# A PEER decoder block: the second product's sums added two PSUM banks at a time, the gate matrix in 8 KB rows and ended earlier, expert numbers and residual moved, 28 lead tiles

## The chip, the cores and the metric

The kernel runs on one core of a Trainium2 chip. The metric is the device time of one execution in microseconds (us); three executions of the kernel before took 3583.12, 3585.42 and 3587.71 us, a median of 3585.42.

## What is computed

One decoder block on 512 tokens of width 2048: two gated token mixers, then a layer of 16384 experts of one neuron each, of which every token takes 8 x 16. The change touches the expert layer, so that part of the reference is shown.

```
def block(xb):                                   # tokens in blocks of 128
    q = (xb @ w_q).reshape(PEER_TOKEN_BLOCK, PEER_HEADS, 2, PEER_HALF)
    s = jnp.einsum('thcd,hcnd->thcn', q, sub_keys).astype(jnp.float32)
    s_top, i_top = lax.top_k(s, PEER_TOPK)
    cand = s_top[:, :, 0, :, None] + s_top[:, :, 1, None, :]
    cand_idx = i_top[:, :, 0, :, None] * PEER_KEYS + i_top[:, :, 1, None, :]
    ...
    best, pos = lax.top_k(cand, PEER_TOPK)
    expert = jnp.take_along_axis(cand_idx, pos, axis=-1)
    gates = jax.nn.softmax(best, axis=-1).astype(xb.dtype)
    u_sel = u_tab[expert]
    v_sel = v_tab[expert]
    act = jax.nn.gelu(jnp.einsum('td,thkd->thk', xb, u_sel))
    return jnp.einsum('thk,thkd->td', gates * act, v_sel)
...
h = rmsnorm(x, norm_ffn[l])
x = x + peer(h, ...)
return rmsnorm(x, norm_final)
```

## The kernel before

**Two ways through the experts.** Of the 512 tokens 160 (GA = 128 and GB = 32) get their experts by row gathers: POOL issues an indirect transfer of one expert row for each of 128 tokens (L963, 1 MB), DVE multiplies and sums it (L1011 for u, L1022 for v, "row" below). The other ND = 352 tokens are computed densely against all 16384 experts, in 128 tiles of 128 experts. Products in float32 are made of three: each weight piece is split by `split` (L204, L205) into a high part, copied by ACT, and a low part, subtracted on DVE or on POOL ("a split" below), and PE adds high x low, high x high and low x high.

**First product.** `dense_u(j)` computes u of tile j: 16 slices x 3 = 48 matmuls of 352 columns into a PSUM bank (L235 to L237), then ACT's gelu (L862) gives ga. The weights of a tile come in two pieces, and so in two splits. For tiles under UPOOL = 10 both are on POOL, later ones on DVE.

**Lead tiles and gate steps.** The first LEAD = 24 tiles are computed ahead; their ga goes to DRAM (d_ga) and comes back later as gar. Meanwhile the gates become a dense matrix. After tile LAG - 1 = 5, `transp_routes` runs the softmax over the scores and turns the chosen expert numbers and gates; from tile LAG on, `gate_steps` issues 88 steps of four tokens. A step is oi and oj on DVE (comparisons of 128 x 512, L892, L898), the multiplication of oi by the gate (every third step on POOL, L894, else on ACT, L897), four token matmuls on PE (L907), and two copies by ACT into a staging tile (L910). After 32 tokens two transfers of 1 MB write the staging tiles to d_g (SP's queue, L913). The steps are spaced so that they end TAIL tiles before the lead does. `pump_rows` issues steps of the row gathers between tiles: RLEAD for each lead tile from LAG + 4 on, RV for each block without a first product.

**Expert numbers.** `expert_ids` makes the numbers (eid) on DVE, after the last top-16. `spread` carries those of the 32 tokens over to 128 partitions: a transfer to d_eb and four back, all on POOL's queue (L823, L825), and likewise the gates through d_gb.

**Second product.** 32 groups of four tiles. `weigh` multiplies ga by the gate: gq is loaded by POOL's queue (L1073), POOL multiplies (L1081), and the result is split into wh (ACT) and wl (DVE). `dense_v(g, dc, ws)` computes one of four blocks dc of the group: 48 matmuls (L1130 to L1132) into four PSUM banks pv, which DVE adds to acc in SBUF one by one (L59, 128 x 352). The pool of pv has six banks. acc begins as the residual, loaded from d_x2 by SP in group 0 (L1120). As long as the tiles of the next group are lead tiles, a group consists of second products only: 20 blocks, of groups 0 to 4. From then on one first product and one block take turns. In the last group `turn_out` turns acc back by transposes into pv banks, ACT squares, DVE multiplies, and `finish` normalises.

**What sets the order.** The program is written engine by engine by a scheduler of the language, which takes instructions by its own estimates of when they can run; `issue_after` ties some to an earlier instruction. Each engine then runs its instructions in the built order, and one that waits holds all that stand behind it. Matmuls, splits and DMA issues stand in such queues, POOL's included.

## Time and profile before

| | |
|---|---|
| median of three executions | 3585.42 us (3583.12 to 3587.71) |
| the profiled execution | 3586.99 us, its span 3584.8 us, mean granted clock 0.98 |
| PE busy | 3416.8 us, 95% |
| DVE busy | 2856.6 us, 80% |
| ACT busy | 1281.7 us, 36% |
| POOL busy | 1452.8 us, 41% |

The times of the stages are counted from the start of the span. PE, DVE, ACT and POOL are the engines for matmuls, vectors, activations and GpSimd; SP only issues transfers. The mixers end about 1330 us; the first product starts before the routing on DVE ends. The gate steps lie between 1434 and 1650 us, the second product starts at 1686 us, and the groups with second products only last until 1897 us. PE records overlap, since matmuls are pipelined: the distance of their starts is what one costs.

### The profile page before, as it was taken

What the parts mean: (1) busy time and instruction counts of PE and PEld (TensorE: products, weight loads), DVE (VectorE), ACT (ScalarE), POOL (GpSimd) and SP (SyncE); (2) the same over time, 40 slices, a digit from 0 to 9 for tenths busy, and PEclk for the clock granted to TensorE, in tenths of its full rate; (3) what the DMA queues carried; (4) which work ended last, traced back from release to release, by engine and by line L of the source; (5) the groups of instructions that cost most, each with busy time, mean ns of one, the idle gap of its engine ahead of it and who ended that gap; (6) DMA issues with size and microseconds to landing.
All of it is one profiled execution on the core that took longest, in us unless ns stands there. A gap on an engine that the chain in (4) does not pass through costs nothing. (4 is left out here: it accounts for less than half of the span.)

```text
span 3584.8 us, 50132 instructions
## 1 busy us (share of the span) xinstructions
PE 3416.8 (95%) x19091; PEld 3169.5 (88%) x19091; DVE 2856.6 (80%) x4147; ACT 1281.7 (36%) x2025; POOL 1452.8 (41%) x924
## 2 busy tenths in 40 slices
PE   8999999999999994997889999999999999999998
PEld 6888888888888884986789999999999999999998
DVE  7685848996535997796866999978999898797984
ACT  4234344325223331873223333333333333433333
POOL 1200000110003543343654666656666666465642
PEclk9999999999999997998899999999999999999999
DMA  5533444434444332699877989898989889897882
GB/s 176 154 108 114 129 123 123 140 125 129 135 147 132 113 111 69 188 302 320 273 252 264 357 333 355 340 337 317 356 347 343 335 342 358 285 361 295 344 303 95
DMA packets 261905, 845.30 MB, mean 236 GB/s; under 512 B 42640, under 2 KB 105184, under 8 KB 219904
## 3 DMA queue, kind: packets, MB, share of 16 engines
q1 hardware_dynamic: 189248, 433.25, 35.9%
q0 software_dynamic: 64352, 396.12, 29.4%
q10 hardware_dynamic: 8064, 12.72, 1.0%
q8 instruction: 150, 2.46, 0.3%
q14 instruction: 91, 0.75, 0.1%
HBM read 790.91 MB, written 51.09 MB: 235 GB/s over the span
## 5 line engine op out<-in xcount | busy, mean ns | idle before, releaser
L204 ACT CAST whi<-wraw 128x1024 fp32r<-128x1024 f32 x736 | 771.9, 1051 | 1792.1 <-PE pu L236 610.5
L205 DVE TENSOR_TENSOR wlo<-wraw,whi 128x1024 fp32r<-128x1024 f32 x556 | 743.1, 1351 | 207.6 <-ACT whi L204 206.5
L237 PE MATMUL pu<-h2h,wlo 128*128 128x352 f32 x2048 | 664.9, 325 | 67.7 <-POOL wlo L205 50.6
L1130 PE MATMUL pv<-wh,whi 128*128 128x352 f32 x2048 | 671.1, 328 | 47.8 <-DVE acc L59 29.9
L1132 PE MATMUL pv<-wh,wlo 128*128 128x352 f32 x2048 | 667.5, 326 | 4.7 <-DVE wlo L205 4.7
L235 PE MATMUL pu<-h2l,whi 128*128 128x352 f32 x2048 | 670.1, 327 | 1.1 <-ACT whi L204 1.1
L1131 PE MATMUL pv<-wl,whi 128*128 128x352 f32 x2048 | 667.5, 326 | 0.0
L236 PE MATMUL pu<-h2h,whi 128*128 128x352 f32 x2048 | 660.2, 322 | 0.0
L205 POOL TENSOR_TENSOR wlo<-wraw,whi 128x1024 fp32r<-128x1024 f32 x180 | 446.9, 2484 | 178.0 <-ACT whi L204 169.8
L1011 DVE SCALAR_TENSOR_TENSOR grow<-grow,rows 128x2048 f32<-128x2048 f32 x160 | 421.2, 2635 | 95.0 <-DMA grow<-in_peer_u_dram,eidx 83.3
L1022 DVE SCALAR_TENSOR_TENSOR rows<-grow,act,rows 128x2048 f32<-128x2048 f32 x160 | 427.8, 2674 | 85.1 <-DMA grow<-in_peer_v_dram,eidx 61.7
L237 PEld LDWEIGHTS pu<-h2h,wlo 128*128 128x128 f32 x2048 | 387.9, 189 | 71.9 <-POOL wlo L205 51.1
L1130 PEld LDWEIGHTS pv<-wh,whi 128*128 128x128 f32 x2048 | 390.9, 191 | 52.0 <-DVE acc L59 33.4
L1132 PEld LDWEIGHTS pv<-wh,wlo 128*128 128x128 f32 x2048 | 390.7, 191 | 5.1 <-DVE wlo L205 5.1
L1131 PEld LDWEIGHTS pv<-wl,whi 128*128 128x128 f32 x2048 | 392.4, 192 | 0.0
L235 PEld LDWEIGHTS pu<-h2l,whi 128*128 128x128 f32 x2048 | 386.8, 189 | 2.4 <-ACT whi L204 1.6
L236 PEld LDWEIGHTS pu<-h2h,whi 128*128 128x128 f32 x2048 | 387.7, 189 | 0.0
L235 PE MATMUL ps<-hl,whi 128*128 128x512 f32 x896 | 353.3, 394 | 9.2 <-ACT whi L204 9.2
L237 PE MATMUL ps<-hh,wlo 128*128 128x512 f32 x896 | 350.8, 392 | 0.4 <-DVE wlo L205 0.4
L236 PE MATMUL ps<-hh,whi 128*128 128x512 f32 x896 | 350.5, 391 | 0.0
L1081 POOL TENSOR_TENSOR ga<-gq,ga 128x352 f32<-128x352 f32 x104 | 171.1, 1646 | 434.8 <-ACT ga L862 418.4
L963 POOL DMA_INDIRECT grow<-in_peer_v_dram,eidx x128 | 247.0, 1930 | 76.5 <-DVE rows L1022 41.4
(338 smaller groups left out, 5084.7 us busy)
## 6 DMA issues: line engine op xcount, KB each, us to landing
wraw<-in_peer_ut_dram SPq DMA_DIRECT2D x256, 512.0 KB
wraw<-in_peer_vt_dram SPq DMA_DIRECT2D x256, 512.0 KB
wraw<-in_w_in_dram SPq DMA_DIRECT2D x112, 512.0 KB
d_g<-stg SPq DMA_DIRECT2D x22, 1024.0 KB
gq<-d_g POOLq DMA_DIRECT2D x32, 704.0 KB, 9.3
wraw<-in_w_vg_dram SPq DMA_DIRECT2D x32, 512.0 KB
wraw<-in_w_out_dram SPq DMA_DIRECT2D x32, 512.0 KB
wraw<-in_w_q_dram SPq DMA_DIRECT2D x32, 512.0 KB
```

The costliest lines, as they stand in the source:

```text
L204: ins = nc.scalar.copy(hi, src).ins
L205: low = (eng or nc.vector).tensor_tensor(lo, src, hi.bitcast(F32), op=ALU.subtract)
L235: nc.tensor.matmul(ps, hi[:, sl], al[k], start=k == 0, stop=False)
L236: nc.tensor.matmul(ps, hi[:, sl], ah[k], start=False, stop=False)
L237: nc.tensor.matmul(ps, lo[:, sl], ah[k], start=False, stop=k == nk - 1)
L963: nc.gpsimd.indirect_dma_start(out=g, out_offset=None, in_=tab, in_offset=bass.IndirectOffsetOnAxis(ap=ids[:, e:e + 1], axis=0))
L1011: nc.vector.scalar_tensor_tensor(g, g, 1.0, x, op0=ALU.mult, op1=ALU.mult, accum_out=act[:, i:i + 1])
L1022: nc.vector.scalar_tensor_tensor(x, g, act[:, i:i + 1], x, op0=ALU.mult, op1=ALU.add)
L1081: pace[0] = nc.gpsimd.tensor_tensor(g3, gq[0][:, :, j % GRP, :], g3, op=ALU.mult).ins
L1130: nc.tensor.matmul(pvs[i], hi[:, s], wh, start=e == 0, stop=False)
L1131: nc.tensor.matmul(pvs[i], hi[:, s], wl, start=False, stop=False)
L1132: nc.tensor.matmul(pvs[i], lo[:, s], wh, start=False, stop=e == GRP - 1)
```

## The change

Six things change together.

- The lead has 28 tiles instead of 24, so 24 blocks of groups 0 to 5 have no first product beside them. The gate steps begin after tile 10 (LAG = 11), and end four tiles before the lead does (TAIL = 4).
- Tiles from UPOOL on split their first piece on DVE and their second on POOL.
- Rows are pumped at 2.0 a lead tile from tile 11 to 24, at 1.2 a block without a first product, and not in group 0.
- d_g is laid out so that a staging tile writes one 8 KB row for each partition; gq's load reads pieces of 512 B as before, now 16 KB apart.
- `spread` of the expert numbers is called in `transp_routes`, after the softmax, instead of right behind `expert_ids`.
- `dense_v` takes two tiles of two banks instead of four of one (three such pairs in the pool), and adds two banks in one instruction of 128 x 704. In group 0 ACT copies the sums into acc, and the residual is loaded in group XG = 4 into a row buffer and added by DVE, four times 128 x 1408.

```diff
@@ -32,18 +32,19 @@
 ND = T - G0
 BLKS = [(0, 128), (128, 128), (256, 96)]
 NE = 128
-LEAD = 24
+LEAD = 28
 TAPS = 10
 P1 = 2.8
 P2 = 4.0
-LAG = 6
+LAG = 11
 GM = 1
-TAIL = 2
+TAIL = 4
 NR = 18
 NROW = 3
-RLEAD = 1.5
-RV = 1.0
+RLEAD = 2.0
+RV = 1.2
 UPOOL = 10
+XG = 4
 GRP = 4
 
 
@@ -173,7 +174,7 @@
     d_x2 = dram.tile([KD, 128, T], F32, name="d_x2")
     d_p = dram.tile([4, 64, 64], F32, name="d_p")
     d_k = dram.tile([32, 32, 128], F32, name="d_k")
-    d_g = dram.tile([ND // 32, NE // GRP, 128, GRP, 32], F32, name="d_g")
+    d_g = dram.tile([ND // 32, 128, NE // GRP, GRP, 32], F32, name="d_g")
     d_eb = dram.tile([GB, 128], I32, name="d_eb")
     d_gb = dram.tile([GB, 128], F32, name="d_gb")
     d_ga = [dram.tile([128, ND], F32, name=f"d_ga{j}") for j in range(LEAD)]
@@ -827,7 +828,6 @@
     eid1 = con2.tile([128, HK], I32, name="eid1")
     expert_ids(eidx, 0)
     expert_ids(eid1, 1)
-    spread(eidb, d_eb, eid1)
     _add(nc, sel, ident[:, 0:GB], ident[:, GB:2 * GB])
     for c in range(2, REP):
         _add(nc, sel, sel, ident[:, c * GB:(c + 1) * GB])
@@ -842,7 +842,7 @@
     gp = gst.enter_context(tc.tile_pool(name="gp", bufs=1, side="right", reuse_waits="tile"))
 
     def ps_v(shape=(512,)):
-        return pp.tile([128, *shape], F32, name="pv", tag="v", bufs=6)
+        return pp.tile([128, *shape], F32, name="pv", tag="v", bufs=3)
 
     def ring(name, dt=F32):
         return rp.tile([128, ND], dt, name=name, tag="ring")
@@ -868,6 +868,7 @@
 
     def transp_routes():
         softmax()
+        spread(eidb, d_eb, eid1)
         spread(gtb, d_gb, gt[:, 1].rearrange("p h k -> p (h k)"))
         for b in range(1, TB):
             lo = max(G0 - b * 128, 0)
@@ -910,8 +911,8 @@
             nc.scalar.copy(stg[q][:, :, u0:u0 + 4], pg[:, q * 64:(q + 1) * 64, :])
         if u0 == 28:
             for q in range(2):
-                nc.sync.dma_start(d_g[t0 // 32, 16 * q:16 * q + 16].rearrange("q i j t -> i q (j t)"),
-                                  stg[q].rearrange("p (q j) t -> p q (j t)", j=GRP))
+                nc.sync.dma_start(d_g[t0 // 32, :, 16 * q:16 * q + 16].rearrange("i q j t -> i (q j t)"),
+                                  stg[q].rearrange("p j t -> p (j t)"))
 
     gars = {}
 
@@ -1051,10 +1052,10 @@
     for j in range(LEAD):
         if j == LEAD - 3:
             gars.update((i, reload(i)) for i in range(GRP))
-        dense_u(j, nc.gpsimd if j < UPOOL else None, gate_steps if j >= LAG else None)
+        dense_u(j, nc.gpsimd if j < UPOOL else (None, nc.gpsimd), gate_steps if j >= LAG else None)
         if j == LAG - 1:
             transp_routes()
-        if j >= LAG + 4:
+        if LAG <= j < LEAD - 3:
             pump_rows(RLEAD)
     gst.close()
 
@@ -1070,7 +1071,7 @@
 
     def load_gates(g):
         gq[0] = accp.tile([128, ND // 32, GRP, 32], F32, name="gq", tag="gq", bufs=1)
-        nc.gpsimd.dma_start(gq[0].rearrange("p b j t -> p b (j t)"), d_g[:, g].rearrange("b i j t -> i b (j t)"))
+        nc.gpsimd.dma_start(gq[0].rearrange("p b j t -> p b (j t)"), d_g[:, :, g].rearrange("b i j t -> i b (j t)"))
 
     def weigh(j, ga):
         if j == 0:
@@ -1116,13 +1117,16 @@
 
     def dense_v(g, dc, ws):
         pcs = []
-        if g == 0:
-            nc.sync.dma_start(acc[:, 4 * dc:4 * dc + 4], d_x2[4 * dc:4 * dc + 4, :, G0:].rearrange("k p t -> p k t"))
+        if g == XG:
+            res = row("res")[:, :4 * ND].rearrange("p (k t) -> p k t", k=4)
+            nc.sync.dma_start(res, d_x2[4 * dc:4 * dc + 4, :, G0:].rearrange("k p t -> p k t"))
+            _add(nc, acc[:, 4 * dc:4 * dc + 4], acc[:, 4 * dc:4 * dc + 4], res)
         for p2 in range(GRP // 2):
             with after(last_wh[0]) if g == 0 and dc else nullcontext():
                 hi, lo = load_w(peer_vt[g, dc, p2], nc.gpsimd if p2 == 1 else None)
             pcs.append((hi, lo))
-        pvs = [ps_v((ND,)) for _ in range(4)]
+        pairs = [ps_v((2, 512)) for _ in range(2)]
+        pvs = [pairs[i // 2][:, i % 2, :ND] for i in range(4)]
         for e, i in [(e, i) for e in range(2) for i in range(4)] + [(e, i) for i in range(4) for e in (2, 3)]:
             hi, lo = pcs[e // 2]
             wh, wl = ws[e]
@@ -1130,15 +1134,18 @@
             nc.tensor.matmul(pvs[i], hi[:, s], wh, start=e == 0, stop=False)
             nc.tensor.matmul(pvs[i], hi[:, s], wl, start=False, stop=False)
             nc.tensor.matmul(pvs[i], lo[:, s], wh, start=False, stop=e == GRP - 1)
-        for i in range(4):
-            a = acc[:, 4 * dc + i]
-            _add(nc, a, pvs[i], a)
+        for h in range(2):
+            a, pv = acc[:, 4 * dc + 2 * h:4 * dc + 2 * h + 2], pairs[h][:, :, :ND]
+            if g == 0:
+                nc.scalar.copy(a, pv)
+            else:
+                _add(nc, a, pv, a)
         if g == NE // GRP - 1:
             turn_out(dc)
 
     ngrp = NE // GRP
     ws_next = [weigh(j, None) for j in range(GRP)]
-    rate = (steps_g - gi[0] - RV * LEAD) / (NE - LEAD - 4)
+    rate = (steps_g - gi[0] - RV * (LEAD - 8)) / (NE - LEAD - 4)
     for g in range(ngrp):
         if g == ngrp - 1:
             for _ in gth:
@@ -1153,7 +1160,7 @@
         ws_next = []
         for dc in range(4):
             jn = (g + 1) * GRP + dc
-            n = 0 if jn >= NE else rate if jn >= LEAD else RV
+            n = 0 if jn >= NE else rate if jn >= LEAD else RV if g else 0
             if jn < NE:
                 ga = dense_u(jn) if jn >= LEAD else None
                 ws_next.append(weigh(jn, ga))
```

The following rows are the built order, engine by engine; line numbers after the change are one higher. Names: wlo is the low part of a split, wraw the weight piece, whi its high part.

First POOL, where the expert numbers pass, before:

```order
L205 TENSOR_TENSOR wlo<-wraw,whi 128x1024 x7
L823 DMA d_eb<-eid_10950 32x128
L205 TENSOR_TENSOR wlo<-wraw,whi 128x1024
L825 DMA eidb<-d_eb 32x32 x4
L205 TENSOR_TENSOR wlo<-wraw,whi 128x1024 x7
L823 DMA d_gb<-gt 32x128
```

and after:

```order
L206 TENSOR_TENSOR wlo<-wraw,whi 128x1024 x7
L824 DMA d_eb<-eid_10954 32x128
L206 TENSOR_TENSOR wlo<-wraw,whi 128x1024
L826 DMA eidb<-d_eb 32x32 x3
L206 TENSOR_TENSOR wlo<-wraw,whi 128x1024
L826 DMA eidb<-d_eb 32x32
L206 TENSOR_TENSOR wlo<-wraw,whi 128x1024 x13
L824 DMA d_gb<-gt 32x128
```

The transfer to d_eb stands behind the same seven splits; between the reads of the numbers and the gates' transfer (d_gb) there were seven splits, and there are now thirteen.

Then POOL at the end of the lead, where the first gq is loaded (oi is a gate multiplication, grow a gathered row, gar a stored ga), before:

```order
L894 TENSOR_TENSOR oi<-oi,tT_10983 128x512
L963 DMA grow<-in_peer_u_dram,eidx 128x2048 x4
L1073 DMA gq<-d_g 128x11x128
L1081 TENSOR_TENSOR gar<-gq,gar 128x352 x4
L205 TENSOR_TENSOR wlo<-wraw,whi 128x1024
L1073 DMA gq<-d_g 128x11x128
```

and after:

```order
L895 TENSOR_TENSOR oi<-oi,tT_10982 128x512 x2
L964 DMA grow<-in_peer_u_dram,eidx 128x2048 x2
L206 TENSOR_TENSOR wlo<-wraw,whi 128x1024
L964 DMA grow<-in_peer_u_dram,eidx 128x2048 x2
L206 TENSOR_TENSOR wlo<-wraw,whi 128x1024
L1074 DMA gq<-d_g 128x11x128
L206 TENSOR_TENSOR wlo<-wraw,whi 128x1024
L1082 TENSOR_TENSOR gar<-gq,gar 128x352 x4
L1074 DMA gq<-d_g 128x11x128
```

Between the last gate multiplication and gq's load there are now splits of lead tiles, and one more stands between the load and the weighing.

Last DVE in a stretch of second products without first ones (grow,act is a row, acc<-pv the sums, wl the low part of a weighed tile), before:

```order
L1011 SCALAR_TENSOR_TENSOR grow,act<-grow,rows_12417 128x2048
L205 TENSOR_TENSOR wlo<-wraw,whi 128x1024
L1011 SCALAR_TENSOR_TENSOR grow,act<-grow,rows_12417 128x2048
L59 TENSOR_TENSOR acc<-pv,acc 128x352 x4
L205 TENSOR_TENSOR wlo<-wraw,whi 128x1024
L205 TENSOR_TENSOR wl<-gar,wh 128x352
```

and after:

```order
L1012 SCALAR_TENSOR_TENSOR grow,act<-grow,rows_12046 128x2048
L60 TENSOR_TENSOR acc<-pv,acc 128x704 x2
L206 TENSOR_TENSOR wlo<-wraw,whi 128x1024
L1012 SCALAR_TENSOR_TENSOR grow,act<-grow,rows_12046 128x2048
L60 TENSOR_TENSOR acc<-pv,acc 128x704 x2
L206 TENSOR_TENSOR wlo<-wraw,whi 128x1024
L206 TENSOR_TENSOR wl<-gar,wh 128x352
```

Two adds of 704 columns stand where four of 352 stood, and a row stands ahead of them as before.

## Rows read from the trace of the kernel before

**Rows 1.** Windows of stages; columns: stretch, length, busy time by engine, clock

```profile
1434.00:1650.00 216.00, 203.98 (x1445) 201.05 (x1446) 190.69 (x230) 162.57 (x460) 91.61 (x54) 0.98 0.81 258
1500.00:1530.00 30.00, 30.00 (x226) 29.98 (x225) 21.81 (x36) 26.41 (x75) 8.65 (x7) 1.00 0.78 243
1560.00:1590.00 30.00, 28.26 (x203) 27.67 (x202) 29.99 (x37) 22.58 (x65) 16.20 (x8) 1.00 0.93 305
1675.30:1719.00 43.70, 21.18 (x99) 20.44 (x99) 22.50 (x22) 9.40 (x15) 26.41 (x18) 0.73 0.84 293
1719.00:1896.90 177.90, 150.37 (x864) 147.06 (x863) 127.15 (x144) 44.86 (x53) 94.34 (x55) 0.94 0.73 248
1896.90:3500.00 1603.10, 1588.27 (x9841) 1583.05 (x9840) 1409.41 (x1240) 534.26 (x645) 971.27 (x521) 0.99 0.88 333
```

**Rows 2.** Timelines of POOL and PE about 1405 us: start, length, instruction, wait.

```profile
1403.73 0.53 POOL L823 DMA_DIRECT2D d_eb<-eid  x1 [54.18 <-DVE eid L819]
...
1406.68 0.66 PE L237 MATMUL pu<-h2h,wlo 128*128 128x352 f32 x1 [48.87 <-POOL wlo L205]
```

**Rows 3.** PE's timeline in the gate stage and at the second product's start.

```profile
1434.05 3.20 PE L907 MATMUL pv<-oj,oi 128*128 128x128 f32 x14 [0.96 <-POOL oi L894]
...
1500.19 1.05 PE L907 MATMUL pv<-oj,oi 128*128 128x128 f32 x8
1500.99 0.41 PE L235 MATMUL pu<-h2l,whi 128*128 128x352 f32 x1
1501.24 0.32 PE L236 MATMUL pu<-h2h,whi 128*128 128x352 f32 x1
1501.40 0.32 PE L237 MATMUL pu<-h2h,wlo 128*128 128x352 f32 x1
...
1649.02 1.05 PE L907 MATMUL pv<-oj,oi 128*128 128x128 f32 x8
...
1685.86 1.54 PE L1130 MATMUL pv<-wh,whi 128*128 128x352 f32 x4 [10.55 <-ACT wh L204]
```

**Rows 4.** DVE's groups, 1440 to 1650: busy us, mean ns, idle before, releaser.

```profile
L892 DVE TENSOR_TENSOR oi<-cs,tT 128x512 f32<-128x512 f32 x82 | 67.6, 825 | 9.4 <-PE pv L907 9.4
L898 DVE TENSOR_TENSOR oj<-cs,tT 128x512 f32<-128x512 f32 x82 | 60.2, 734 | 0.0
L205 DVE TENSOR_TENSOR wlo<-wraw,whi 128x1024 fp32r<-128x1024 f32 x24 | 33.9, 1411 | 10.2 <-ACT whi L204 10.2
L1011 DVE SCALAR_TENSOR_TENSOR grow<-grow,rows 128x2048 f32<-128x2048 f32 x14 | 32.5, 2339 | 3.6 <-DMA grow<-in_peer_u_dram,eidx 3.6
```

**Rows 5.** ACT's timeline at the gelu of tile 5.

```profile
1424.61 0.46 ACT L862 ACTIVATE ga<-pu 128x352 f32<-128x352 f32 x1
```

**Rows 6.** POOL's groups, 1440 to 1650.

```profile
L894 POOL TENSOR_TENSOR oi<-oi,tT 128x512 f32<-128x512 f32 x28 | 48.2, 1723 | 101.2 <-DVE oi L892 101.2
...
L205 POOL TENSOR_TENSOR wlo<-wraw,whi 128x1024 fp32r<-128x1024 f32 x4 | 10.6, 2668 | 0.2 <-ACT whi L204 0.2
```

**Rows 7.** Timelines of POOL and DVE about 1545 us.

```profile
1544.76 1.33 POOL L894 TENSOR_TENSOR oi<-oi,tT 128x512 f32<-128x512 f32 x1 [3.51 <-DVE oi L892]
...
1545.12 1.52 DVE L892 TENSOR_TENSOR oi<-cs,tT 128x512 f32<-128x512 f32 x1
```

**Rows 8.** Timelines of SP and POOL behind the last gate step.

```profile
1653.13 12.71 SPq L913 DMA_DIRECT2D d_g<-stg  x2
...
1674.66 1.16 POOL L1073 DMA_DIRECT2D gq<-d_g  x1 [15.52 <-issue]
```

**Rows 9.** Waits, 1719 to 1897: total us, times, longest.

```profile
PE pv L1130 <- DVE acc L59: 27.5, 11, 5.2
```

**Rows 10.** DVE's groups, 1719 to 1897.

```profile
L1011 DVE SCALAR_TENSOR_TENSOR grow<-grow,rows 128x2048 f32<-128x2048 f32 x18 | 45.5, 2527 | 27.2 <-DMA grow<-in_peer_u_dram,eidx 27.2
L59 DVE TENSOR_TENSOR acc<-pv,acc 128x352 f32<-128x352 f32 x72 | 33.9, 513 | 8.8 <-PE pv L1132 8.8
```

**Rows 11.** DVE's timeline in the last turns.

```profile
3542.33 1.88 DVE L51 TENSOR_TENSOR ost<-pv,gfb 128x512 f32<-128x512 f32 x3
```

## The prediction

> **What bounds the kernel now.** I first read the busy time by stage. From 1896.9 us to 3500 us PE is busy 1588.3 of 1603.1 us at clock 0.99: there PE is the bound, and the change leaves its number of matmuls alone. The loss lies earlier: the gate stage (1434.0 to 1650.0), the start of the second product (1675.3 to 1719.0, PE busy 21.2 of 43.7, clock 0.73) and the twenty blocks that hold second products only (to 1896.9) [rows 1]. Ahead of all this stands one long wait: POOL waits 54.18 us for the expert numbers, and PE 48.87 us for the half weight that is queued behind on POOL [rows 2].
>
> In the gate stage both PE and DVE matter. At 1500 to 1530 PE is busy throughout and DVE 21.8 of 30; at 1560 to 1590 DVE is busy 29.99 of 30 and PE 28.3 [rows 1]. So first PE is the bound, and once rows are mixed in, DVE.
>
> **Prices.** Matmuls of 352 columns start 0.16 us apart (1501.24, 1501.40), so 48 take 7.7. A gate step of four tokens starts at 1500.19, the next matmul at 1500.99, the one after 0.25 later: 0.80 plus 0.09, so 0.89 [rows 3]. On DVE: oi 0.825, oj 0.734, a split 1.411, a row 2.339 [rows 4].
>
> **Expert numbers later.** The source moves them, the built order on POOL does not: the transfer to d_eb still stands behind the same splits and waits for the same conversion, and DVE's order is the same up to there. The 48.87 us stay: 0.
>
> **The lead.** The gates start behind tile 10 instead of tile 5. Tile 5's gelu is at 1424.61 [rows 5], the first gate token at 1434.05 [rows 3], 9.44 later. Five more tiles at 7.7 put tile 10's gelu at 1463.1, the first token at 1472.6, and one more split on DVE ahead of the softmax sums (1.4) at 1474.
>
> Next, the length of the gate stage. The count is from the built orders, between first and last gate step. PE: 88 steps in both, 724 matmuls of u before, 577 after. DVE: 88 oi and oj in both, 23 splits and 13 rows before, 11 splits and 21 rows after. PE before 88 x 0.89 + 724 x 0.16 + 16 turns x 0.12 = 196.0, after 172.5. DVE before 88 x 1.559 + 23 x 1.411 + 13 x 2.339 + 9 for a norm = 209.1; its busy time is 190.7 [rows 1], since records overlap by some 0.08 us, so I scale by 0.912. After 137.2 + 15.5 + 49.1 + 9 = 210.8, scaled 192.3. DVE has no less to do: twelve splits go, eight rows come. Since the bound changes hands, I take the larger of the two in blocks of eight steps: before 207.2 (five blocks by PE, six almost all by DVE), after 191.7 (DVE but for the first two). The 216.0 measured are 8.8 above the first sum, and I keep 8.8.
>
> Seven more splits lie on POOL in this stage (11 against 4), of 2.67 us each [rows 6]. They can slow DVE: the oi at 1545.12 took 1.52 beside a POOL multiply from 1544.76 to 1546.09 [rows 7], against a mean of 0.825. The mean gives less: oi lasts 0.091 longer than oj, 82 times, 7.5 us for 48.2 us of POOL multiplies [rows 4, 6], 0.4 for one split. Bounds are nothing and 2.67; I take 1.0, nearer to the mean, so 7.
>
> Stage after: 191.7 + 8.8 + 7 = 207.5, end at 1681.5. Behind it come 198 matmuls of u, 31.7, since no rows are pumped in the last three tiles: lead end 1713.2. Before, 24 tiles ended at 1675.3, and four more at 7.7 make 1706.0. **Plus 7.2** (-9, if the 8.8 and the 7 are not there, to 19, if POOL stops DVE for each split's whole length).
>
> **The second product's start.** Before, the last gate token is at 1649.02, the first matmul of the product at 1685.86 after 10.55 us of waiting [rows 3]. Between lie the last d_g write, whose issue alone holds SP for 12.71 us, and gq's issue on POOL, at 1674.66 after 15.52 us of waiting [rows 8]: 36.8 us. Of the 43.7 us to 1719.0, 96 matmuls are 15.4, so 28.3 are lost [rows 1]. After, 31.7 us of matmuls lie between the last token and the lead's end, and a row of d_g is one piece of 8 KB where it was sixteen of 512 B, so SP should issue it in less. At worst 5 remain, I take 3. If the cover is gone because POOL reaches gq late (it now stands ahead of one split for the last lead tile), the whole 28 come back. The four copies that ACT does in the first group stand behind wh splits that wait for the next gq: 1 each, 4.
>
> **The blocks with second products only.** They become 24 from 20. The 18 blocks to 1896.9 lasted 177.9 for 138.2 of matmuls: 39.7 lost, 2.2 a block [rows 1]. 27.5 of it is PE waiting for DVE's adds, eleven times [rows 9]; ahead of the adds on DVE stand rows, for whose gathers it waits 27.2 us [rows 10]. Now the pairs. A block's first bank is finished 2.88 us before its end and was needed by the next block 0.96 after its start; less the add of 0.51 [rows 10] DVE may be 3.3 us late. A pair is finished 1.92 before the end and is needed 0.96 after. Its add of 704 columns is no row of this trace: between 0.76 (0.513 at 352 and 0.627, the third of 1.88, at 512 [rows 10, 11] carried on) and twice 0.513; I take 0.9. That leaves 2.0. Eleven waits of 1.3 more are 14.3 in 18 blocks, 0.8 a block; 1.2 rows a block instead of 1.0 add up to 0.5. Some of it is hidden, since a late PE gives DVE time: I take 2.8 a block, with bounds of 1.3 and 4.0. The residual adds of 1408 columns are 1408/2048 of a row, 1.6 each; of four I count 4 us together (0 to 6.4).
>
> Lost after: 3 + 4 + 4 + 20 x 2.8 = 67, before 28.3 + 39.7 = 68. **Minus 1.**
>
> **The rest.** The pool's three pairs also serve the last turns, where six banks did; ACT's square and DVE's multiply (0.63) [rows 11] now hold the next block: plus 3 (0 to 8). Rows per block in the long stage rise from 2.91 to 2.96 and gq is read in pieces 16 KB apart: plus 1 (0 to 6, as the DMA share is 0.88 [rows 1]). **Plus 4.**
>
> **Sum.** 7.2 - 1 + 4 = +10.2 on the profiled execution of 3586.99, whose span is 3584.8: 3597.2. That execution lies 1.6 above the median, so 3595.6, or **3595**. With r for the loss in a block the whole change is 20r - 45.8: everything hangs on r and on the start.
>
> **Rivals.** What a measurement of this kernel can tell from no change is about 0.2%, 7.2 us, so r from 1.9 to 2.7 is no change.
>
> *The splits on POOL stop DVE for their whole length.* 7 x 2.67 = 18.7 instead of 7: +22 in all, 3607. The one oi that lasted 1.52 speaks for it [rows 7], the mean of 82 against [rows 4]. The Trainium skill ("SBUF — State Buffer", section "Who interferes with whom") says just this: DVE with two inputs in SBUF and GpSimd reading SBUF share a read port that is locked for an instruction's length, and the later one blocks. By that rule the split on POOL is no gift to DVE, and the single row agrees with it.
>
> *The pairs cost much more.* If DVE is late in nearly every block, r = 4: +34, 3619.5. For it: DVE is busy 127.2 of 177.9 us there [rows 1]. Against it: 72 adds become 36 longer ones.
>
> *No change.* r stays 2.2, since the waits come from rows that land late and not from a lack of banks: 20 x 2.2 - 45.8 = -1.8, 3583.6. For it: 27.2 of waiting for gathers against 27.5 of waiting for adds [rows 9, 10].
>
> *Faster: the gathers land in time.* The long writes of d_g no longer hold SP (12.71 us for the last two [rows 8]), and the four loads of the residual, 704 KB each, leave the start. If DVE then does not wait for rows, the waits for adds go: r falls towards (39.7 - 27.5)/18 = 0.7; at 1.3, half way, the sum is -19.8, 3565.6. It decides from r below 1.9. Against it: the DMA share in these blocks is 0.73 only [rows 1], so the gathers are late by their place in the queue rather than by load.
>
> *The change does what it says on the expert numbers,* and the stall of 48.87 goes: 10.2 - 48.9 = -38.7, 3546.7. Against it the built order.
>
> **How the numbers follow.** Forecast 0.42 (of which 0.09 within the bound), splits on POOL 0.08, dear pairs 0.10, no change 0.17, gathers in time 0.20, stall gone 0.03. Faster: 0.20 + 0.03 = 0.23; the same: 0.17 + 0.09 = 0.26; slower: 0.33 + 0.08 + 0.10 = 0.51. The range from 3565 to 3620 leaves out the stall's case, some half of the faster one, and the far side of the dear pairs, some 0.18. Around the forecast itself it is 3588 to 3607.
>
> **What would show it.** POOL still waits some 54 us at the transfer to d_eb, and PE 49. First gate token near 1474, last near 1681, lead end near 1713; DVE busy over 90% between. The first matmul of the product then follows within 3 us. PE's wait for the adds grows from 27.5 to some 45 us in 20 blocks. Wrong it is if DVE is not the bound in the gate stage, if gq's issue comes after the lead's end, or if the waits for adds shrink.

## The result and the profile after

The changed kernel takes 3641.52 us in the median (3637.64 to 3648.2), the kernel before 3586.57: a ratio of 1.0155, 95% interval 1.0135 to 1.0176. It is 55 us slower; the forecast was 10 us slower, and the range ended at 3620. The profiled execution has a span of 3636.3 us against 3584.8, so 51.5 us are to be found in its trace. (The 3586.57 is the median of the three executions of the kernel before and a fourth.)

The stages of the kernel after. The columns are stretch, length, busy time of PE, PEld (PE's weight loading), DVE, ACT and POOL with counts, granted clock, DMA share, GB/s: the gate stage, the rest of the lead, the groups with second products only, the long stage.

```profile
1472.80:1697.26 224.46, 189.49 (x1290) 184.75 (x1291) 217.26 (x235) 155.18 (x452) 113.72 (x68) 0.93 0.71 264
1697.26:1741.70 44.44, 36.40 (x208) 35.24 (x206) 16.01 (x13) 10.50 (x15) 22.77 (x15) 0.92 0.93 344
1741.70:2002.80 261.10, 207.95 (x1152) 201.98 (x1153) 169.22 (x147) 69.41 (x87) 132.85 (x79) 0.92 0.71 245
2002.80:3500.00 1497.20, 1479.01 (x9191) 1475.71 (x9190) 1315.46 (x966) 494.67 (x595) 894.88 (x492) 1.00 0.90 337
```

In the gate stage DVE is now busy 217 of 224 us, where it was 191 of 216 [rows 1], and PE waits for DVE's splits, 28.4 us in place of 8.6 before (1472 to 1697; total us, times, longest):

```profile
PE pu L238 <- DVE wlo L206: 28.4, 10, 4.8
```

The marks of all runs, from PE's timeline: first gate token, end of the last, end of the lead's matmuls, first matmul of the second product, end of the groups without first products, span.

| run | first token | last token | lead end | product | groups end | span |
|---|---|---|---|---|---|---|
| before | 1434.1 | 1650.1 | 1675.3 | 1685.9 | 1896.9 | 3584.8 |
| after | 1472.8 | 1698.3 | 1741.7 | 1742.6 | 2002.8 | 3636.3 |
| e1, after, splits on DVE | 1469.5 | 1679.1 | 1723.9 | 1724.8 | 1984.3 | 3632.5 |
| e2, after, numbers late | 1441.1 | 1666.1 | 1704.5 | 1705.5 | 1965.9 | 3608.2 |
| e3, before, pairs | 1433.8 | 1650.7 | 1674.5 | 1682.1 | 1900.2 | 3593.6 |
| e4, before, 28 lead tiles | 1469.4 | 1671.7 | 1718.4 | 1719.3 | 1968.2 | 3598.3 |
| e5, before, splits on POOL | 1432.8 | 1673.1 | 1690.6 | 1705.8 | 1918.7 | 3601.3 |
| e6, before, d_g in 8 KB rows | 1432.7 | 1649.4 | 1677.1 | 1684.0 | 1896.3 | 3586.7 |
| e7, before, numbers late | 1427.2 | 1644.1 | 1669.2 | 1679.7 | 1895.2 | 3580.8 |
| e9, before, numbers late, 28 lead tiles | 1441.2 | 1644.7 | 1688.7 | 1689.7 | 1939.0 | 3570.0 |
| e11, after, no rows in lead | 1471.7 | 1650.0 | 1688.3 | 1689.2 | 1940.1 | 3660.1 |
| e12, after, no rows in lead's end | 1471.0 | 1689.3 | 1729.8 | 1730.7 | 1987.8 | 3643.7 |
| e13, after, last tile on DVE | 1470.6 | 1696.7 | 1732.5 | 1733.5 | 1996.8 | 3636.2 |
| e14, before, numbers late, LAG 8 | 1429.7 | 1633.9 | 1651.2 | 1669.7 | 1880.0 | 3566.8 |

Where the 51.5 us went, with 7.68 us (48 x 0.16) for each further tile or block:

| | before | after | difference | forecast |
|---|---|---|---|---|
| lead end, with four more tiles before | 1706.0 | 1741.7 | +35.7 | +7.2 |
| groups without first products, above their matmuls | 68.0 | 76.8 | +8.8 | -1 |
| the rest, with four tiles and four blocks fewer | 1626.5 | 1633.5 | +7.0 | +4 |

The lead holds most of it. Its start came as forecast. The stall stands where it was, in the rows that answer to [rows 2], and the gelu of tile 10 and the first token came at 1463.40 and 1472.84, forecast 1463.1 and 1474. The timelines of POOL, PE, ACT and PE:

```profile
1403.90 0.53 POOL L824 DMA_DIRECT2D d_eb<-eid  x1 [54.19 <-DVE eid L820]
...
1406.85 0.66 PE L238 MATMUL pu<-h2h,wlo 128*128 128x352 f32 x1 [48.76 <-POOL wlo L206]
...
1463.40 0.46 ACT L862 ACTIVATE ga<-pu 128x352 f32<-128x352 f32 x1
...
1472.84 2.95 PE L908 MATMUL pv<-oj,oi 128*128 128x128 f32 x24 [0.18 <-ACT oi L898]
```

From there the stage lasted 225.5 us to the end of the last token, not 207.5. These are DVE's groups of the stage, 1473 to 1697, with mean ns and idle time before (they answer to [rows 4]):

```profile
L893 DVE TENSOR_TENSOR oi<-cs,tT 128x512 f32<-128x512 f32 x86 | 89.9, 1045 | 5.3 <-PE pv L908 4.2 <-POOL oi L895 1.0
L899 DVE TENSOR_TENSOR oj<-cs,tT 128x512 f32<-128x512 f32 x86 | 65.3, 759 | 0.0
L1012 DVE SCALAR_TENSOR_TENSOR grow<-grow,rows 128x2048 f32<-128x2048 f32 x22 | 56.9, 2588 | 0.0
L206 DVE TENSOR_TENSOR wlo<-wraw,whi 128x1024 fp32r<-128x1024 f32 x12 | 16.8, 1398 | 0.0
```

and this is POOL's of the splits, which answers to [rows 6]:

```profile
L206 POOL TENSOR_TENSOR wlo<-wraw,whi 128x1024 fp32r<-128x1024 f32 x11 | 28.2, 2568 | 3.7 <-ACT whi L205 3.5
```

The counts are those of the built order, the prices are not those of before: oi went from 825 to 1045 ns, rows from 2339 to 2588. With them DVE's sum is 88 x 1.804 + 11 x 1.398 + 21 x 2.588 + 9 = 237.5, times 0.915 the 217.3 that it was busy. The forecast had 192.3 plus 7.

### The profile page after: what moved, and what is told of

Same layout as the page of the kernel before. It is cut to its first block, busy times and chain, and to the rows that moved or that the text cites. A ratio compares the mean times of both kernels' runs of the same rounds, so it can differ in the third digit from the quotient of the medians.

```text
span 3636.3 us, 49886 instructions
## 1 busy us (share of the span) xinstructions
PE 3433.5 (94%) x19091; PEld 3179.3 (87%) x19091; DVE 2828.7 (78%) x3869; ACT 1287.4 (35%) x2033; POOL 1455.8 (40%) x942
## 3 DMA queue, kind: packets, MB, share of 16 engines
q1 hardware_dynamic: 147584, 433.98, 35.7%
## 5 line engine op out<-in xcount | busy, mean ns | idle before, releaser
L206 DVE TENSOR_TENSOR wlo<-wraw,whi 128x1024 fp32r<-128x1024 f32 x538 | 702.8, 1317 | 261.2 <-ACT whi L205 260.2
L206 POOL TENSOR_TENSOR wlo<-wraw,whi 128x1024 fp32r<-128x1024 f32 x198 | 492.5, 2488 | 235.2 <-ACT whi L205 232.8
L1023 DVE SCALAR_TENSOR_TENSOR rows<-grow,act,rows 128x2048 f32<-128x2048 f32 x160 | 444.5, 2778 | 79.2 <-DMA grow<-in_peer_v_dram,eidx 58.6
L1082 POOL TENSOR_TENSOR ga<-gq,ga 128x352 f32<-128x352 f32 x100 | 151.9, 1519 | 429.9 <-ACT ga L862 411.5
L964 POOL DMA_INDIRECT grow<-in_peer_v_dram,eidx x128 | 232.9, 1819 | 78.2 <-DVE rows L1023 50.2
```

The source lines that it names most:

```text
L206: low = (eng or nc.vector).tensor_tensor(lo, src, hi.bitcast(F32), op=ALU.subtract)
L964: nc.gpsimd.indirect_dma_start(out=g, out_offset=None, in_=tab, in_offset=bass.IndirectOffsetOnAxis(ap=ids[:, e:e + 1], axis=0))
L1023: nc.vector.scalar_tensor_tensor(x, g, act[:, i:i + 1], x, op0=ALU.mult, op1=ALU.add)
L1082: pace[0] = nc.gpsimd.tensor_tensor(g3, gq[0][:, :, j % GRP, :], g3, op=ALU.mult).ins
```

## The experiments on the lead

**The splits on POOL, taken away after the change (e1).** The changed kernel with lead tiles from 10 on split on DVE alone:

```diff
-        dense_u(j, nc.gpsimd if j < UPOOL else (None, nc.gpsimd), gate_steps if j >= LAG else None)
+        dense_u(j, nc.gpsimd if j < UPOOL else None, gate_steps if j >= LAG else None)
```

> The changed kernel, but lead tiles from 10 on are split on DVE alone, as before the change. Two theories for the gate stage, which lasted 224.4 us after the change where 207.5 was forecast. Theory P: a split on POOL (2.57 us, 11 in the stage) holds DVE for nearly its whole length, which is why oi went from 825 to 1045 ns and rows from 2339 to 2588. Then 12 more splits on DVE cost 12 x 1.4 x 0.91 = 15 us and the 11 splits gone from POOL give 24 back: gate stage some 216 us, oi again near 830 ns, total some 8 to 12 us under the changed kernel's 3641.5. Theory R: the eight more rows made the stage long, and POOL's splits relieve DVE. Then the stage grows by some 10 us to 234, total 3650.

Measured 3632.06 us (3625.33 to 3634.31), 9.5 less than the changed kernel in the medians. The gate stage fell from 225.5 to 209.6 (1469.5 to 1679.1). DVE's groups there, 1472 to 1690:

```profile
L893 DVE TENSOR_TENSOR oi<-cs,tT 128x512 f32<-128x512 f32 x84 | 72.6, 865 | 4.5 <-PE pv L908 4.5
L899 DVE TENSOR_TENSOR oj<-cs,tT 128x512 f32<-128x512 f32 x84 | 57.8, 688 | 0.0
L1012 DVE SCALAR_TENSOR_TENSOR grow<-grow,rows 128x2048 f32<-128x2048 f32 x22 | 54.7, 2512 | 0.0
L206 DVE TENSOR_TENSOR wlo<-wraw,whi 128x1024 fp32r<-128x1024 f32 x25 | 31.1, 1247 | 0.0
```

DVE has twice the splits and the stage is 15.9 us shorter, which is theory P: the twelve splits cost DVE some 14 us (12 x 1.247 x 0.915), so the eleven on POOL had cost the stage some 30, about their own 28.2. oi is back near its time of before; the rows are not (2512), so the splits are not what made them dearer: in both runs they take 2.28 us, or 3.12 to 3.13 beside a gate multiplication on POOL.

The single instructions show the price directly, where the means of [rows 4] hide it. In the kernel before 72 of 86 oi and 84 of 86 oj last 0.67 to 0.69 us. The four splits on POOL [rows 6] ran beside two other oi and the two other oj. POOL's and DVE's timelines:

```profile
1454.00 5.15 POOL L205 TENSOR_TENSOR wlo<-wraw,whi 128x1024 fp32r<-128x1024 f32 x2
1463.16 5.44 POOL L205 TENSOR_TENSOR wlo<-wraw,whi 128x1024 fp32r<-128x1024 f32 x2 [0.15 <-ACT whi L204]
...
1454.24 2.65 DVE L892 TENSOR_TENSOR oi<-cs,tT 128x512 f32<-128x512 f32 x1 [1.11 <-PE pv L907]
1456.82 2.88 DVE L898 TENSOR_TENSOR oj<-cs,tT 128x512 f32<-128x512 f32 x1
1459.62 0.68 DVE L892 TENSOR_TENSOR oi<-cs,tT 128x512 f32<-128x512 f32 x1
...
1463.48 2.88 DVE L898 TENSOR_TENSOR oj<-cs,tT 128x512 f32<-128x512 f32 x1
1466.28 2.87 DVE L892 TENSOR_TENSOR oi<-cs,tT 128x512 f32<-128x512 f32 x1
```

So each split cost DVE 2.0 to 2.2 us already before the change. After it, all eleven splits of the stage run beside one longer instruction of DVE (seven oi, two oj, a split and a norm), 24.5 us longer in sum. Two of them:

```profile
1517.98 2.81 POOL L206 TENSOR_TENSOR wlo<-wraw,whi 128x1024 fp32r<-128x1024 f32 x1
1536.65 2.38 POOL L206 TENSOR_TENSOR wlo<-wraw,whi 128x1024 fp32r<-128x1024 f32 x1
...
1518.49 2.85 DVE L893 TENSOR_TENSOR oi<-cs,tT 128x512 f32<-128x512 f32 x1
1536.34 3.24 DVE L893 TENSOR_TENSOR oi<-cs,tT 128x512 f32<-128x512 f32 x1
```

Of the 17.8 us by which the lead ended earlier the profiled execution gave 14.7 back in its long stage (1648 us against 1633.5). No part of the edit lies there; PE's waits for DVE's splits are longer (9.1 and 6.4 us against 2.9 and 5.3), and why is not settled.

**The same edit alone, on the kernel before (e5).**

```diff
-        dense_u(j, nc.gpsimd if j < UPOOL else None, gate_steps if j >= LAG else None)
+        dense_u(j, nc.gpsimd if j < UPOOL else (None, nc.gpsimd), gate_steps if j >= LAG else None)
```

> The kernel before, with one edit: lead tiles from 10 on split their second piece on POOL. Between first and last gate step DVE then has 12 splits instead of 23 and POOL 16 instead of 4. Theory P (a POOL split holds DVE for its length): DVE loses 11 x 1.41 x 0.91 = 14 us of own work and gets 12 x 2.6 x 0.9 = 28 us of standing, gate stage 216 to some 228 us, total 3586.6 to some 3597. Theory R (POOL splits relieve DVE): gate stage some 207 us, total some 3578.

Measured 3609.2 us (3603.1 to 3612.17), ratio 1.0069 (1.0052 to 1.0086): slower by 24 us, twice what theory P had said. The gate stage is 240.3 us. Three groups, 1434 to 1650, on DVE and POOL:

```profile
L892 DVE TENSOR_TENSOR oi<-cs,tT 128x512 f32<-128x512 f32 x80 | 76.4, 955 | 10.4 <-PE pv L907 9.1 <-ACT oi L897 1.3
...
L1011 DVE SCALAR_TENSOR_TENSOR grow<-grow,rows 128x2048 f32<-128x2048 f32 x13 | 35.6, 2748 | 12.6 <-DMA grow<-in_peer_u_dram,eidx 12.6
...
L205 POOL TENSOR_TENSOR wlo<-wraw,whi 128x1024 fp32r<-128x1024 f32 x15 | 40.9, 2735 | 10.9 <-ACT whi L204 10.6
```

DVE's instructions are longer again, and here DVE is not even full: it is busy 186 of these 216 us. What adds to the standing is POOL's queue. Gate multiplications stand behind splits that wait for ACT (10.6 us), PE waits 7.9 us for such an oi in this stretch, and for the last token another 5.02. DVE also waits 12.6 us for gathers, which POOL issues from the same queue, where it was 3.6 [rows 4]. How much each of these adds is not separated. A split handed to POOL is thus paid on DVE and in POOL's order.

The Trainium skill ("SBUF — State Buffer", section "Who interferes with whom") states the lock on the shared read port. The trace after agrees with it: 24.5 us on DVE for 28.2 us of splits. That the later one blocks, as the prediction has it from there, is not borne out: in five of the eleven pairs, that at 1536 among them, DVE's record begins 0.3 us before POOL's, and it is DVE's that is long.

**The lead's schedule alone, on the kernel before (e4).**

```diff
-LEAD = 24
+LEAD = 28
-LAG = 6
+LAG = 11
-TAIL = 2
+TAIL = 4
...
-        if j >= LAG + 4:
+        if j >= 10:
```

> The kernel before with LEAD 28, LAG 11, TAIL 4 only (rows pumped from tile 10 on at 1.5 as before; in the gate stage 23 splits and 16 rows on DVE, no split on POOL). By the prediction's sum with these counts: gate stage (137.2 + 32.5 + 37.4 + 9) x 0.912 = 197 of DVE, about 206 us; lead end 6 us later than four more tiles would put it; second product starts at once, which gives 25 us; four more blocks at 2.2 cost 9: total some 10 us under before, 3576. If instead a late start of the gates is what costs (DVE as the bound from first step to last, the last tiles' weights late), the lead ends 20 us or more late and the total is 3590 or more.

Measured 3600.3 us (3598.35 to 3602.76), ratio 1.0042 (1.0028 to 1.0056): the second case. The gate stage was as forecast for these counts, 202.3 us against 206, and the product's start cost nothing (0.93 us). But from the last token's end to the lead's end it took 46.8 us for 31.7 us of matmuls. ACT's and PE's timelines there:

```profile
1702.57 1.04 ACT L204 CAST whi<-wraw 128x1024 fp32r<-128x1024 f32 x1 [21.05 <-DMA wraw<-in_peer_ut_dram]
...
1703.67 0.66 PE L235 MATMUL pu<-h2l,whi 128*128 128x352 f32 x1 [9.67 <-ACT whi L204]
...
1719.34 0.91 PE L1130 MATMUL pv<-wh,whi 128*128 128x352 f32 x4 [0.93 <-ACT wh L204]
```

The weights of a lead tile landed 21 us after ACT was free for them: from 1680 to 1719 the windows show a DMA share of 1.04 to 1.05, with gate rows, gathers and the next weights at once. So the bubble of [rows 3] before the second product is gone, but of its 28.3 us 15.1 are back in this stretch, 9.67 of them the wait for these weights.

**The end of the lead after the change.** There the same stretch took 43.4 us. PE waited for DVE's split (2.89) and twice for POOL's (5.1). POOL's and PE's timelines:

```profile
1717.82 1.16 POOL L1074 DMA_DIRECT2D gq<-d_g  x1 [8.95 <-DMA d_ga<-ga]
1720.74 2.77 POOL L206 TENSOR_TENSOR wlo<-wraw,whi 128x1024 fp32r<-128x1024 f32 x1 [1.77 <-ACT whi L205]
1727.97 4.61 POOL L1082 TENSOR_TENSOR gar<-gq,gar 128x352 f32<-128x352 f32 x4 [4.46 <-DMA gq<-d_g]
1732.88 1.12 POOL L1074 DMA_DIRECT2D gq<-d_g  x1 [0.30 <-DMA d_ga<-ga]
1734.03 4.67 POOL L206 TENSOR_TENSOR wlo<-wraw,whi 128x1024 fp32r<-128x1024 f32 x2
...
1736.43 0.66 PE L238 MATMUL pu<-h2h,wlo 128*128 128x352 f32 x1 [4.92 <-POOL wlo L206]
```

The last lead tile's second piece is the first of the two splits at 1734: it stands behind the weighing, which waits for gq. Two runs tell this apart from late transfers. The first (e12) pumps no rows behind the gate steps:

```diff
-        if LAG <= j < LEAD - 3:
+        if LAG <= j < LEAD - 7:
```

> The changed kernel with rows pumped only up to seven tiles before the lead's end (20 instead of 28): no row stands behind the last gate step. Theory D: behind the last gate step the DMA engines are the bound (share about 1.0 from 1700 to 1730, weights 11.4 us late), and four gathers of 1 MB are a quarter of what they carry. Then the 31.7 us of matmuls take some 35 instead of 43.4, of which 4.9 is the wait for POOL's split behind gq; the gate stage has three rows less, 218. The eight rows come back in the long stage at about 3 us each: total some 3650. Rival: the weights are late by SP's order alone, and the stretch stays at 43 us.

Measured 3641.36 us (3637.02 to 3645.66), no change. The stretch took 40.4 us at a DMA share of 0.73:

```profile
1689.30:1729.70 40.40, 33.84 (x199) 33.32 (x197) 4.90 (x4) 10.49 (x14) 16.16 (x11) 0.92 0.73 254
```

and PE's one wait in it was 6.6 us for POOL's split. With the DMA engines relieved the stretch is hardly shorter, so theory D falls for the changed kernel. The lead ended 11.9 us earlier, the long stage with eight rows more took 22 longer. The second run (e13) splits the last tile on DVE alone:

```diff
-        dense_u(j, nc.gpsimd if j < UPOOL else (None, nc.gpsimd), gate_steps if j >= LAG else None)
+        dense_u(j, nc.gpsimd if j < UPOOL else (None, nc.gpsimd if j < LEAD - 1 else None), gate_steps if j >= LAG else None)
```

> The changed kernel with the last lead tile split on DVE alone. PE waited 4.92 us for that tile's second piece, which stands on POOL behind the weighing and the next gq. Theory: this wait goes, and the product's start with it comes 5 us earlier, 3636. Rival: the start then waits for gq and the weighing instead and nothing changes, 3641.

Measured 3635.57 us (3633.03 to 3649.39). The stretch took 35.8 us, 7.6 less, at a granted clock of 1.00 and a DMA share of 1.02:

```profile
1696.70:1732.50 35.80, 32.09 (x199) 31.25 (x197) 18.04 (x13) 10.49 (x14) 18.97 (x12) 1.00 1.02 388
```

PE waits 3.7 us in it instead of 8.0, and its records take 32.1 us instead of 35.4, at the granted clock of 1.00 in place of 0.92. So POOL's order held this end of the lead. Another queue can do the same: in e1, with no split of these tiles on POOL, the stretch took 44.8 us, and PE waited for a split on DVE that stands behind rows whose gathers came late. DVE's and PE's timelines of e1:

```profile
1691.36 2.29 DVE L1012 SCALAR_TENSOR_TENSOR grow<-grow,rows 128x2048 f32<-128x2048 f32 x1 [9.05 <-DMA grow<-in_peer_u_dram,eidx]
...
1698.89 0.66 PE L238 MATMUL pu<-h2h,wlo 128*128 128x352 f32 x1 [9.77 <-DVE wlo L206]
```

The total of e13 moved as expected in the medians, but within the scatter of the runs, and the profiled span is no shorter than after the change (3636.2): its later stages took the gain back.

**Rows out of the lead (e11).** The changed kernel with no rows pumped in the lead:

```diff
-RLEAD = 2.0
+RLEAD = 0.0
```

> The changed kernel without any rows pumped during the lead (RLEAD = 0); the long stage then takes some 0.29 rows a block more. Theory: rows cost the lead twice, on DVE (21 x 2.59 x 0.915 = 50 us of the gate stage's 217 busy) and on the DMA engines (share about 1.0 behind the last gate step, where weights came 11.4 us late and the 31.7 us of matmuls took 43.4). Then the gate stage shortens from 224 to some 185, bound by PE and the POOL splits, the rest of the lead to some 34, the lead ends some 48 us earlier, and if the long stage has room on DVE (88% busy) the total is some 3594. Rival: the rows cost the same where they go, total within 15 us of 3641.

Measured 3660.49 us (3649.22 to 3667.57). The lead did what the theory said: it ended at 1688.3 instead of 1741.7, with a gate stage of 178.3. But the long stage took 1720 us instead of 1633.5, 3.1 us for each of the 28 rows. PE's wait in the long stage, 2000 to 3660 (total us, times, longest):

```profile
PE pu L238 <- DVE wlo L206: 50.4, 22, 4.2
```

After the change this wait was 2.9 us in two places. The long stage is bound by PE only as long as DVE just keeps up; at 3.25 rows a block instead of 2.96 it does not. The rows in the lead were cheap where they were.

## The experiments on the other parts

**The pairs alone, on the kernel before (e3)**, with the copies by ACT and the residual in group 4:

```diff
-        return pp.tile([128, *shape], F32, name="pv", tag="v", bufs=6)
+        return pp.tile([128, *shape], F32, name="pv", tag="v", bufs=3)
...
-        pvs = [ps_v((ND,)) for _ in range(4)]
+        pairs = [ps_v((2, 512)) for _ in range(2)]
+        pvs = [pairs[i // 2][:, i % 2, :ND] for i in range(4)]
...
-        for i in range(4):
-            a = acc[:, 4 * dc + i]
-            _add(nc, a, pvs[i], a)
+        for h in range(2):
+            a, pv = acc[:, 4 * dc + 2 * h:4 * dc + 2 * h + 2], pairs[h][:, :, :ND]
+            if g == 0:
+                nc.scalar.copy(a, pv)
+            else:
+                _add(nc, a, pv, a)
```

> The kernel before with the second product's part of the change only: pairs of banks (three in the pool), adds of 704 columns, ACT copies in group 0, residual added in group 4. By the prediction: PE's wait for the adds grows from 1.5 to some 2.1 us a block in the blocks with second products only, +11, the last turns +3, residual adds +4, and the start is no better since the gates end as before: total some 3600. The rival, that pairs cost nothing since the waits come from late rows: within 5 us of 3586.6.

Measured 3595.59 us (3590.25 to 3599.29), ratio 1.0027 (1.0017 to 1.0036). By its trace the groups without first products lost 4 us more and the rest 5.5. In the stretch of [rows 9], 1719 to 1900, PE waits 28.3 us for DVE's adds eleven times, as before. The wait did not grow in this run: 17 rows waited 16.9 us for their gathers, where 18 had waited 27.2 [rows 10].

After the change it did grow. DVE's groups from 1760 to 2003, which answer to [rows 10]:

```profile
L1012 DVE SCALAR_TENSOR_TENSOR grow<-grow,rows 128x2048 f32<-128x2048 f32 x25 | 71.3, 2856 | 50.3 <-DMA grow<-in_peer_u_dram,eidx 50.3
L60 DVE TENSOR_TENSOR acc<-pv,acc 128x704 f32<-128x704 f32 x39 | 33.4, 881 | 10.5 <-PE pv L1136 10.5
...
L60 DVE TENSOR_TENSOR acc<-acc,res 128x1408 f32<-128x1408 f32 x4 | 7.0, 1755 | 2.3 <-DMA res<-d_x 2.3
```

and the wait of PE from 1741.7 to 2002.8 (total us, times, longest), which answers to [rows 9]:

```profile
PE pv L1134 <- DVE acc L60: 43.4, 14, 5.9
PE pv L1134 <- ACT acc L1140: 6.6, 2, 5.3
```

The add of 704 columns is 0.881 us, forecast 0.9; the waits are 43.4 us, forecast some 45. But the forecast took their growth from the shorter time that a pair leaves DVE, and the gathers have changed too: DVE waits 50.3 us for them in 25 rows, where it was 27.2 in 18. How much of the growth each made is not shown; the pairs alone (e3) made none. The second line is PE's wait for ACT's copies in group 0.

**The layout of d_g alone (e6)**, on the kernel before; the slices of the writes and of gq's load follow the new order as in the change:

```diff
-    d_g = dram.tile([ND // 32, NE // GRP, 128, GRP, 32], F32, name="d_g")
+    d_g = dram.tile([ND // 32, 128, NE // GRP, GRP, 32], F32, name="d_g")
```

> The kernel before with the layout of d_g only: staging tiles written in rows of 8 KB, gq read in pieces of 512 B that lie 16 KB apart. The prediction priced it at nothing. SP was held 3.4 to 12.7 us by each pair of writes before; if weights of the lead were late for that, the gate stage and the start shorten by up to 10 us (3577). If the reads of gq become dearer, 32 groups of up to 1 us add (3600). No effect: within 5 us of 3586.6.

Measured 3586.75 us (3583.43 to 3593.05), ratio 1.0005 (0.9995 to 1.0015): nothing, as priced. SP was held 0.8 to 1.1 us by each pair of writes, where it was 2.1 to 12.7.

**The expert numbers really later (e2).** In the changed kernel the transfer is tied to POOL's last split:

```diff
         softmax()
-        spread(eidb, d_eb, eid1)
+        with after(pace[0]):
+            spread(eidb, d_eb, eid1)
```

> The changed kernel with the transfer of the expert numbers tied to POOL's last split of tile 10, so that in the built order it stands behind twenty splits instead of seven. The changed kernel still waited 54.19 us on POOL at that transfer and 48.76 us on PE. Theory S: this wait lies on the path, and all behind it moves up by it: gate stage from about 1425 us, total 3641.5 - 45 = some 3596. Rival: the wait only changes its place (the gate steps need the same numbers, which DVE has at about 1404 us, and top-16 on DVE gets slower beside POOL's splits): less than 20 us gained, 3622 or more.

Measured 3613.13 us (3609.99 to 3618.29), 28 less than after the change: between the two. PE's timeline shows what is late next:

```profile
1420.44 0.66 PE L238 MATMUL pu<-h2h,wlo 128*128 128x352 f32 x1 [18.41 <-DVE wlo L206]
```

Tile 10's first piece is split on DVE, behind the numbers, and these came later than before. The kernel of the next run shows it on POOL's timeline, where fifteen splits lie between 1340 and 1397 instead of three:

```profile
1422.41 0.53 POOL L823 DMA_DIRECT2D d_eb<-eid  x1 [25.81 <-DVE eid L819]
```

That run (e9) is the kernel before with the numbers later, 28 lead tiles (LAG 11, TAIL 4) and d_g in 8 KB rows; the edits are those above.

> The kernel before with LEAD 28, LAG 11, TAIL 4, the expert numbers really later (behind the splits of tile 10) and d_g in 8 KB rows; single banks, splits on DVE, residual first and 1.5 rows from tile 10 on stay as before. With the lead alone it was 3600.3; without the stall of 48.8 us some 3552, if the gates can start by 1425 us. If top-16 on DVE, which ends at 1403, is what the start waits for, some 3570.

Measured 3577.61 us (3572.1 to 3586.6), ratio 0.9981 (0.9971 to 0.999), above both values expected. DVE's routing, the top-16 and the expert numbers behind it, ended at 1422 instead of 1403.7, 18.7 us later, beside twelve more splits on POOL (29 us). Not all of DVE's instructions became longer. POOL's and DVE's timelines of e9, with a comparison of two inputs and a reduction of one, each beside a split:

```profile
1359.65 2.40 POOL L205 TENSOR_TENSOR wlo<-wraw,whi 128x1024 fp32r<-128x1024 f32 x1 [1.34 <-ACT whi L204]
1363.49 2.41 POOL L205 TENSOR_TENSOR wlo<-wraw,whi 128x1024 fp32r<-128x1024 f32 x1 [1.45 <-ACT whi L204]
...
1359.97 2.62 DVE L793 TENSOR_TENSOR oh<-pf,cs 128x512 f32<-128x512 f32 x1
1363.59 0.66 DVE L798 TENSOR_REDUCE ij<-oh 128x32 f32<-128x512 f32 x1
```

The mean of these comparisons went from 682 ns in the kernel before to 1373, that of the reductions stayed at 674. The stall had a use: it kept POOL off DVE.

**The numbers later and nothing else (e7)**, on the kernel before, by the same two lines and without the call behind `expert_ids`:

> The kernel before with the expert numbers really later (the transfer tied to POOL's last split of tile 5) and nothing else. PE then goes on through tile 5 to some 1376 us, and the gates wait for the numbers on DVE: top-16 ended at 1403, and four more POOL splits beside it cost some 1.6 us each (12 of them moved it by 19). First gate token at some 1420 instead of 1434, all else behind it 14 us earlier: 3572. Rival: what was hidden under the stall comes out and nothing is gained, 3586.

Measured 3580.0 us (3576.66 to 3583.28), ratio 0.9988 (0.9978 to 0.9997). The first token came at 1427.2, 7 us earlier and not 14: the numbers came at 1409, and PE waited 8.08 us for a split that POOL begins behind the transfers.

**With two more tiles in that wait (e14).** The same, with

```diff
-LAG = 6
+LAG = 8
...
-        if j >= LAG + 4:
+        if j >= 10:
```

> As the run with the numbers alone, but with LAG 8 (LEAD 24, TAIL 2 as before): two more tiles fill PE's wait. The numbers come at some 1412, the first gate token at some 1428; between first and last gate step PE has 628 matmuls of u instead of 724 and DVE the same work, so the stage is bound by DVE, some 207 us. Lead end at 1428 + 207 + 25 = 1660 instead of 1675: 3571. If the later start eats what the fuller PE brings, it is no better than LAG 6.

Measured 3566.4 us (3565.37 to 3568.92), ratio 0.9944 (0.9927 to 0.9961): the fastest of all, 17 us under before and 75 under the changed kernel. First token at 1429.7 as expected (1428), gate stage 204.2 (207), lead end at 1651.2, 24 us earlier than before. Eight of them are lost again at the product's start, where PE waits 18.51 us for the first wh instead of 10.55.

## Why the prediction was wrong, point by point

The profiled execution became 51.5 us longer and not 10.2. Of the 41.3 us between, 18.0 lie in the gate stage, 11.7 between the last token and the lead's end, 9.8 in the groups without first products and 3.0 in the rest; the lead's start gave 1.2 back.

- **The stall stays:** right. 54.19 and 48.76 us, and the built order had told it. What e2, e7 and e9 add: a call that is moved in the source must also be tied to something if the scheduler is to move it, and of the 48.8 us some 28 are then to be had.
- **The lead's start:** right, 1472.8 against 1474.
- **The price of a split on POOL:** the step that failed. The sum took 1.0 us of DVE for each of seven more. The trace after gives 24.5 us for eleven, 2.2 each, and by e1 the stage lost some 30, about the splits' whole length. The value was chosen by the mean of oi over [rows 4, 6], less that of oj. But 72 of 86 oi were not held at all, and two of the oj taken as the measure were. Each of the four splits of before had already cost DVE 2.0 to 2.2 us, in rows of the same trace that the sum did not use. The single row [rows 7] was the one to follow. The rival of this name had the mechanism; it had 0.08, and its 3607 priced the seven in place of the 1.0 and left the rest of the stage as it was. Stage: 225.5 measured, 207.5 forecast. By these rows seven more splits cost 15.9 us (24.5 less 8.6), 8.9 above the 7 of the sum; the 21 rows at 2588 ns instead of 2339 add 5.2, and the other 4 of the 18.0 are not assigned.
- **31.7 us of matmuls behind the last token:** failed too. It took 43.4, and the step named no resource for it. PE waited 8.0 us for splits in it, 4.92 of them for the last tile's, behind gq and the weighing in POOL's queue, and its records took 35.4 us at a granted clock of 0.92. Without that split on POOL 7.6 of the 11.7 us too many were gone (e13). The prediction had seen this split and used it only for the start.
- **The product's start:** right. 0.93 us of waiting in place of 10.55.
- **The blocks without first products:** 76.8 us lost against 67. The add (0.881, forecast 0.9), the wait for the adds (43.4, some 45) and ACT's copies in group 0 (6.6, 4) came near the forecast. That the wait did is partly luck: the gathers came later too, and the pairs alone did not lengthen it (28.3 in e3, 27.5 before), so the mechanism is not shown.
- **The rest:** 7.0 against 4, within its bounds. In the last turns PE waits 4.9 us for DVE where it did not before, and e3 has the same. Layout of d_g: nothing, right.
- **Sum of the parts.** Splits on POOL +24, the lead's schedule +15, pairs +10, layout 0, each alone on the kernel before, in the medians: 49 of the 55 us. The parts do not simply add, so this agreement is partly chance: taken out of the changed kernel, the splits on POOL gave 9.5 us back and not 24. The rows' rates and the move of `spread` alone were not run.

The range was too narrow because its upper end took the POOL splits and the dear pairs as cases that exclude each other (both together would have been 3631), and no case for the lead's end. None of the three signs that the prediction named for being wrong came: DVE was the bound in the gate stage, gq was issued at 1717.8, ahead of the lead's end, and the waits for adds grew.

## What to carry to other kernels

Work moved from a full engine to an idle one is only free if the two do not share a port: price it by single rows in which both were at work, not by a mean that is mostly made of rows that ran alone. In an engine that runs in order, ask for every instruction that is handed to it what it will stand behind at the end of the stage as well. And before a wait is removed, look at what it kept apart: here the stall kept POOL's splits away from the routing on DVE.

## What the runs showed of the hardware

- A comparison of 128 x 512 on DVE takes 0.68 us. Beside a gate multiplication on POOL (1.3 us) it took 1.52 [rows 7], beside a subtraction of 128 x 1024 on POOL (2.4 to 2.8 us) 2.65 to 3.26. A reduction on DVE, with one input, took 0.66 us beside such a subtraction (e9), where the mean in the kernel before is 0.674.
- Writing 1 MB in rows of 8 KB for each partition held SP 0.34 us per transfer in the median (0.38 in e6), in sixteen pieces of 512 B 1.07, and 0.38 to 12.1. It did not change the total.
